# A plan of side pieces between an expert's twelve blocks of matmuls, and the first expert's tables spread over its blocks

## The chip, the core and the metric

One core of a Trainium2 chip runs the whole layer as one program. The metric is the device time of one execution in microseconds. The kernel before takes 2020.53 us, the median of three runs (2020.08 to 2022.52).

## What is computed

One layer over 1024 latent tokens of width 1024 and 256 context tokens: a mixer (gated linear attention and pooling) and then a mixture of 32 experts, four to a token. The change touches the experts alone:

```python
def moe(h, w_router, b_router, w_gu, b_gu, w_down, b_down):
    logits = (xt @ w_router + b_router).astype(jnp.float32)
    top_vals, top_idx = lax.top_k(logits, TOP_K)
    weights = jax.nn.softmax(top_vals, axis=-1)
    ...                                        # tokens sorted by expert, in blocks of 128
    def expert_block(args):
        xblk, e = args
        gu = xblk @ w_gu[e] + b_gu[e]          # 1024 -> 2048
        gate, up = jnp.split(gu, 2, axis=-1)
        gate = jnp.minimum(gate, SWIGLU_LIMIT)
        up = jnp.clip(up, -SWIGLU_LIMIT, SWIGLU_LIMIT)
        act = (up + 1.0) * gate * jax.nn.sigmoid(SWIGLU_ALPHA * gate)
        return act @ w_down[e] + b_down[e]     # 1024 -> 1024
    ...                                        # weighted sum back to the tokens
```

All is float32, and `h + g2 * moe(...)` with a last RMSNorm is the output.

## The kernel before, in words

**Blocks.** An expert's weights are a stream of twelve loads of 1 MB: eight of `w_gu` (128 rows by 2048) and four of `w_down` (256 rows by 1024). SyncE issues them into eight buffers (`ring`, `mix`, `ringx` in the rows). ScalarE rounds each load to `hl[:, 0]` and VectorE writes the remainder to `hl[:, 1]` (`split`, lines 131 and 132), in three `hl` buffers; so the split of a block can start only when TensorE is done with the block three before it. A block of matmuls is then twelve matmuls of 128 by 512 (`gu_chunk` writes `pG`, `dn_chunk` writes `pD`). The eight gate/up blocks of expert e are followed by the four down blocks of expert e-1, and that is one turn of the loop at the end of the listing. The activation of e (`act`, lines 1533 to 1536: `ag` and `at`) is worked out during those four down blocks.

**Heavy and light experts.** An expert has a main set of 128 token slots. The sixteen with the most tokens, here called heavy, have one more set of 32 (the first of them two); the rest are light. A heavy expert's further set adds unsplit matmuls (`pR`) behind its gate/up blocks 3 and 7 and behind its last down block. In the order of work the experts go H H H L L H, then L H twelve times, then L L.

**Side pieces.** Between blocks TensorE does small work for the neighbouring experts: `prep_x` transposes the gathered tokens of the next expert (parts 0 and 1, four transposes each into `pps`, evacuated by a ScalarE copy and a VectorE subtraction into `xT`; part 2, two transposes into `ppr`, evacuated by one ScalarE copy, for a heavy one only), `prep_a` does the same for the activations (`aT`, `aqT`), and `prep_route` finds the token numbers of the expert after next (`pq`) and starts their gather on GpSimd. All of these, and the tables below, share one PSUM bank: the pool `ptr`, tag `t`, one buffer. A piece therefore waits until the piece before it has been evacuated. Before, the pieces stand behind fixed gate/up blocks:

```python
A_AT, X_AT = (0, 2, 3), (4, 6, 7)
```

for the parts 0, 1, 2 of `prep_a` and of `prep_x`; `prep_sel` (VectorE) is written behind block 6, and `prep_route` behind the second down block.

**Start of the experts.** After `prep_x` of the first expert, the bias table (`bias_rows`: three matmuls and a ScalarE copy for each of four quarters), the routing weights (`route_weights`) and the slot weights of two experts follow one after the other, each through the same bank, and then the first block. Behind the first expert's blocks stands `route_blocks`, a chain of small VectorE operations with two small groups of matmuls (`pcs`, `pblk`), and then the second expert begins.

**Order.** A scheduler orders the instructions of VectorE, ScalarE and GpSimd by its own estimate of when each is ready. TensorE's are kept in the order of the program from the expert loop on (`T.strict`).

Of the kernel before, what the change touches and what calls it, by code (L numbers as in the profile page):

```python
# [9 lines left out]
F32 = mybir.dt.float32  # L10
# [4 lines left out]
AF = mybir.ActivationFunctionType  # L15
# [4 lines left out]
P = 128  # L20
D = 1024
KT = D // P
# [4 lines left out]
NE = 32  # L27
# [8 lines left out]
MAXBLK = 32  # L36
# [16 lines left out]
def tile_hybrid_layer(ctx: ExitStack, tc: tile.TileContext, x, c, ctx_in, c_ctx, w_ada, b_ada, norm_mix_w,  # L53
# [9 lines left out]
    V, S, G = nc.vector, nc.scalar, nc.gpsimd  # L63

    def dump(name, ap):
        if name in dbg:
            nc.sync.dma_start(dbg[name], ap)
# [263 lines left out]
    todo = []  # L331
# [895 lines left out]
    def route_weights():  # L1227

        flat = lg.rearrange("p t e -> p (t e)")
        S.activation(lgn, lg, AF.Copy)  # L1230
        G.tensor_tensor(bdg, bdg, g2b[0:96], op=ALU.mult)
        px = ptr.tile([P, 2, P], F32, name="px", tag="t")
        for h in range(2):
            T.transpose(px[:, h], flat[:, h * P:(h + 1) * P], ident)
        wT = tp.tile([P, 2, P], F32, name="wT")
        S.activation(wT, px, AF.Copy)
        py = ptr.tile([P, 2, P], F32, name="pyw", tag="t")
        for h in range(2):
            T.matmul(py[:, h], wT[:, h], pbd.rearrange("p j e -> p (j e)"), start=True, stop=True)
        V.tensor_copy(flat, py.rearrange("p h r -> p (h r)"))  # L1240
        eq = tp.tile([P, NT, NE], F32, name="eq")
        S.activation(info[:, :, :, 2], lg, AF.Copy)
        V.tensor_tensor(eq, lg, info[:, :, :, 2], op=ALU.subtract)
        S.activation(info[:, :, :, 3], eq, AF.Copy)
        V.tensor_tensor(eq, eq, info[:, :, :, 3], op=ALU.subtract)
        S.activation(info[:, :, :, 4], eq, AF.Copy)
        for j in range(4):
            S.activation(g2r[32 * j:32 * j + 32], g2b[32 * j:32 * j + 32, 256 * j:256 * j + 256], AF.Copy)

    def route_blocks():  # L1250

        erb = tp.tile([NE, 2 * NE + 1], F32, name="erb")
        V.tensor_copy(erb[:, 0:NE], pe_[:NE, 0:NE])
        nb = tp.tile([NE, 1], F32, name="nb")
        tmp1 = tp.tile([NE, 1], F32, name="tmp1")
        over = tp.tile([NE, 1], F32, name="over")
        pcs = ptr.tile([NE, 8], F32, name="pcs", tag="t")
        T.matmul(pcs[:, 0:1], eqr[:NE], cnt[:NE], start=True, stop=True)
        V.tensor_tensor(over, pcs[:, 0:1], cap4, op=ALU.subtract)
        for j in range(7):  # L1260
            dst = nb if j == 0 else tmp1
            V.tensor_scalar(dst, over, float(P * j), None, op0=ALU.is_gt)
            if j:
                V.tensor_tensor(nb, nb, tmp1, op=ALU.add)
        pb = ptr.tile([P, 3, NE], F32, name="pblk", tag="t")
        nbb = tp.tile([NE, 2, MAXBLK], F32, name="nbb")
        V.tensor_copy(nbb[:, 0], nb.to_broadcast([NE, MAXBLK]))
        V.tensor_copy(nbb[:, 1], capc.to_broadcast([NE, MAXBLK]))
        T.matmul(pb[:MAXBLK, 0], nbb[:, 0], linc, start=True, stop=True)
        T.matmul(pb[:MAXBLK, 1], nbb[:, 0], ident[:NE, :NE], start=True, stop=True)  # L1270
        T.matmul(pb[:MAXBLK, 2], nbb[:, 1], ident[:NE, :NE], start=True, stop=True)
        inc = tp.tile([MAXBLK, 3, NE], F32, name="inc")
        V.tensor_copy(inc, pb[:MAXBLK])
        V.tensor_copy(nblk1[:, 0:1], inc[0:1, 0, NE - 1:NE])
        V.tensor_scalar(nblk1[:, 1:2], inc[0:1, 0, NE - 1:NE], 1.0, None, op0=ALU.min)
        le = tp.tile([MAXBLK, NE], F32, name="le")
        V.tensor_scalar(le, inc[:, 0], pcol[:MAXBLK], None, op0=ALU.is_le)
        rb_ = tp.tile([MAXBLK, 1], F32, name="rb_")
        V.tensor_reduce(rb_, le, axis=mybir.AxisListType.X, op=ALU.add)
        V.tensor_tensor(le, le, inc[:, 1], op=ALU.mult)  # L1280
        first = tp.tile([MAXBLK, 1], F32, name="first")
        V.tensor_reduce(first, le, axis=mybir.AxisListType.X, op=ALU.add)
        row = tp.tile([MAXBLK, 136], F32, name="row")
        V.memset(row, 0.0)
        V.tensor_scalar(row[:, 0:NE], io[:MAXBLK, 0:NE], rb_, None, op0=ALU.is_equal)
        capb = tp.tile([MAXBLK, 1], F32, name="capb")
        V.tensor_tensor(le, row[:, 0:NE], inc[:, 2], op=ALU.mult)
        V.tensor_reduce(capb, le, axis=mybir.AxisListType.X, op=ALU.add)
        eb = tp.tile([MAXBLK, 1], F32, name="eb")
        V.tensor_tensor(le, row[:, 0:NE], erb[:, 0:NE], op=ALU.mult)  # L1290
        V.tensor_reduce(eb, le, axis=mybir.AxisListType.X, op=ALU.add)
        for i in range(3):
            V.tensor_scalar(row[:, (i + 1) * NE:(i + 2) * NE], io[:MAXBLK, 0:NE], eb, None, op0=ALU.is_equal)
        V.tensor_tensor(first, pcol[:MAXBLK], first, op=ALU.subtract)
        V.scalar_tensor_tensor(row[:, 4 * NE:4 * NE + 1], first, float(P), capb, op0=ALU.mult, op1=ALU.add)
        ebi = tp.tile([MAXBLK, 1], I32, name="ebi")
        V.tensor_copy(ebi, eb)
        nc.scalar.dma_start(ovt, row)
        nc.scalar.dma_start(ove, ebi)
# [11 lines left out]

    bq = ap.tile([P, 4, 512], BF16, name="bq", tag="bq")

    def bias_rows():
        perm = ap.tile([P, 2 * D], BF16, name="perm", tag="y")[:, 0:1536].rearrange(
            "p (a q n j i) -> p a q n j i", a=3, q=4, n=4, j=8)
        V.memset(perm, 0.0)
        for i in range(3):
            V.tensor_copy(perm[:, i, :, :, :, i], pbd.rearrange("p n (q j) -> p q n j", q=4))
        for q in range(4):  # L1320
            pb = ptr.tile([P, 512], F32, name="pbq", tag="t")
            for i in range(3):
                T.matmul(pb, perm[:, i, q].rearrange("p n j i -> p (n j i)"), bt[:, i], start=(i == 0), stop=(i == 2))
            S.activation(bq[:, q], pb, AF.Copy)

    slots = RS + [MS[0], MS[2], MS[3]] + RX

# [64 lines left out]
    def slot_weights(i, pq):  # L1392
        n = 1 + nrem[i]
        wc = xp.tile([P, 3], F32, name="wc", tag="wc", bufs=4)
        V.tensor_reduce(wc[:, :n], pq[:, :n, 2:5], axis=mybir.AxisListType.X, op=ALU.add)
        R["wc", i] = wc

    def prep_route(i):
        pq = ptr.tile([P, 3, 8], F32, name="pq", tag="t")
        route_main(i, pq, slice(0, 5))  # L1400
        route_rem(i, pq, slice(2, 7))
        gather_main(i, pq)
        gather_rem(i, pq)
        slot_weights(i, pq)
# [290 lines left out]
    with tc.high_priority():  # L1695
# [18 lines left out]
        pinned[0] = False  # L1714
        for p_ in range(3):
            prep_x(0, p_)
    bias_rows()
    route_weights()
    dump("posm", posm)
    dump("wfull", lg)  # L1720
    for i in range(2):
        pq = ptr.tile([P, 3, 8], F32, name="pq", tag="t")
        route_main(i, pq, slice(2, 5))
        route_rem(i, pq, slice(2, 5))
        slot_weights(i, pq)
    T.strict = True
    A_AT, X_AT = (0, 2, 3), (4, 6, 7)
    for e in range(nexp + 1):
        if e < nexp:
            gu_start(e)  # L1730
            for k in range(KT):
                advance()
                gu_chunk(e, k)

                if e > 0 and k in A_AT:
                    prep_a(e - 1, A_AT.index(k))
                if e + 1 < NE and k in X_AT:
                    prep_x(e + 1, X_AT.index(k))
                if e + 2 < NE and k == 6:
                    prep_sel(e + 2)  # L1740
                if e + 2 < NE and k == 7 and e == 0:
                    prep_route(e + 2)
        if e > 0:
            dn_start(e - 1)
            for k0 in range(0, KT, 2):
                advance()
                with tc.high_priority() if e == NE - 1 else ExitStack():
                    if k0 == 0 and e < nexp:
                        act(e)
                    if e == NE - 1 and k0 >= 4:  # L1750
                        prep_a(e, k0 // 2 - 2)
                dn_chunk(e - 1, k0)
                if k0 == 2 and e + 2 < NE:
                    prep_route(e + 2)
                if e == NE:
                    (final_tables, lambda: final_weights(0), lambda: final_weights(1), int)[k0 // 2]()
            finish_e(e - 1)
            if e == NE - 1:
                prep_a(e, 2)
                final_rows()  # L1760
        elif nexp:
            act(e)
            route_blocks()
# [149 lines left out]
```

## Time and profile before

| | |
|---|---|
| median of three runs | 2020.53 us |
| profiled execution, its own time | 2023.95 us |
| its span, first to last instruction | 2022.2 us |
| TensorE (PE) busy | 1872.5 us, 93% |
| VectorE (DVE) busy | 1544.6 us, 76% |
| ScalarE (ACT) busy | 1139.1 us, 56% |
| mean granted TensorE clock | 0.971 |

The span is that of one profiled execution, and some 1.8 us lie around it. The experts begin at about 558 us and end at about 1990 us. A share over the whole span mixes the mixer, where TensorE often waits, with the experts, where it seldom does; the rows below are therefore taken from stretches of the experts. In a timeline row, the bracket at the end is the idle time of the engine just before the row, with what ended it.

### The profile page before, as it was taken

Reading aid. Unit: us, or ns where it says so; the run is one execution under the profiler, and the core shown is the slowest. Engines: PE = TensorE matmul, PEld = TensorE weight load, DVE = VectorE, ACT = ScalarE, POOL = GpSimd, SP = SyncE. Lnnn points to the kernel's source line nnn. Section 1 sums busy time; section 2 is a strip of 40 time slices with the busy share of each in tenths; the row PEclk is TensorE's granted clock in tenths of the full one; section 3 lists DMA queues with packets and bytes.
Section 4 is the critical chain, followed back from the end, with each engine's and each line's share of the span. In section 5 each row is a group of like instructions: output and inputs, shape, how many; then the busy total and the mean of one; then the engine's idle time right before and its main releaser. Section 6 shows DMA issues by size and latency. Waiting matters only on the chain.

```text
span 2022.2 us, 29473 instructions
## 1 busy us (share of the span) xinstructions
PE 1872.5 (93%) x11472; PEld 1373.6 (68%) x11473; DVE 1544.6 (76%) x1606; ACT 1139.1 (56%) x1267; POOL 339.0 (17%) x238
## 2 busy tenths in 40 slices
PE   7999998999389999999999999999999999999995
PEld 4776776787256677767677676767667676767774
DVE  5486478658667788878788788878878887887887
ACT  4564456644435566656566565656656565665664
POOL 2010043011300221111111111111111111111114
PEclk9999998999599999999999999999999999999998
DMA  9285422243635789968888796888879688887985
GB/s 343 78 295 180 152 75 92 77 151 134 237 159 199 285 327 332 357 248 355 297 317 326 283 367 246 348 305 316 324 286 366 246 343 302 322 324 290 365 305 178
DMA packets 125528, 532.33 MB, mean 263 GB/s; under 512 B 13196, under 2 KB 27328, under 8 KB 90568
## 3 DMA queue, kind: packets, MB, share of 16 engines
q1 hardware_dynamic: 109464, 481.82, 61.2%
q0 software_dynamic: 15344, 48.01, 9.1%
q8 instruction: 92, 1.51, 0.3%
q10 hardware_dynamic: 576, 0.56, 0.1%
q14 instruction: 52, 0.43, 0.1%
HBM read 497.68 MB, written 32.67 MB: 262 GB/s over the span
## 4 chain that ended last, share of the span: by engine, by line
PE 78%; DVE 9%; ACT 5%; issue 4%; DMA 3%; POOL 1%; SPq 0%; POOLq 0%; DVEq 0%; ACTq 0%
PE pG L74 31%; PE pD L74 17%; PE pa L74 12%; PE pR L74 9%; ACT hl L131 4%; DVE hl L132 3%; PE pw L74 2%; PE pps L79 2%; PE pt L74 2%; DMA ringx<-in_w_down_dram 1%; PE pt L79 1%; PE ppr L79 1%; PE pDl L74 1%; PE pq L74 1%; DVE xT L1413 1%
## 5 line engine op out<-in xcount | busy, mean ns | idle before, releaser
L74 PE MATMUL pG<-hl,xT 128*128 128x512 f32 x3072 | 769.2, 402 | 0.0
L74 PEld LDWEIGHTS pG<-hl,xT 128*128 128x128 f32 x3072 | 566.0, 189 | 144.3 <-issue 21.9
L132 DVE TENSOR_TENSOR hl<-ring,hl 128x2048 fp32r<-128x2048 f32 (+2 forms) x199 | 398.4, 2009 | 168.9 <-ACT hl L131 167.4
L131 ACT ACTIVATE hl<-ring 128x2048 fp32r<-128x2048 f32 (+2 forms) x199 | 331.9, 1670 | 304.2 <-PE pG L74 168.2
L132 DVE TENSOR_TENSOR hl<-mix,hl 128x2048 fp32r<-128x2048 f32 x144 | 329.5, 2290 | 121.8 <-ACT hl L131 121.8
L131 ACT ACTIVATE hl<-mix 128x2048 fp32r<-128x2048 f32 (+1 forms) x146 | 277.7, 1902 | 234.4 <-PE pG L74 168.7
L74 PE MATMUL pD<-hl,aT 128*128 128x512 f32 x1488 | 365.5, 401 | 0.3 <-DVE hl L132 0.3
L74 PEld LDWEIGHTS pD<-hl,aT 128*128 128x128 f32 x1488 | 276.6, 189 | 76.0 <-issue 11.7
L132 DVE TENSOR_TENSOR hl<-ringx,hl 128x2048 fp32r<-128x2048 f32 x96 | 219.7, 2288 | 24.5 <-ACT hl L131 24.2
L131 ACT ACTIVATE hl<-ringx 128x2048 fp32r<-128x2048 f32 x96 | 184.0, 1917 | 93.0 <-PE pG L74 54.5
L1374 POOL DMA_INDIRECT xg<-h2d,ix x32 | 64.4, 2012 | 884.3 <-DVE ix L1370 424.8
L74 PE MATMUL pa<-hl,hi 128*128 128x512 f32 x544 | 180.4, 417 | 5.7 <-DVE wsg L760 3.7
L1588 POOL DMA_INDIRECT acc<-y,ix x31 | 104.5, 3369 | 156.8 <-DVE y L1583 156.8
L74 PEld LDWEIGHTS pa<-hl,hi 128*128 128x128 f32 x544 | 102.5, 197 | 31.4 <-DVE wsg L760 4.8
L74 PE MATMUL pa<-hl,lo 128*128 128x512 f32 x272 | 107.7, 407 | 0.0
L74 PE MATMUL pa<-hi,hl 128*128 128x512 f32 (+1 forms) x288 | 95.6, 395 | 1.0 <-ACT hi L400 1.0
L74 PEld LDWEIGHTS pa<-hi,hl 128*128 128x128 f32 x288 | 54.9, 193 | 16.2 <-ACT hi L400 2.9
L1593 POOL DMA_INDIRECT acc<-yq,ixr x17 | 34.0, 1999 | 163.5 <-DMA acc<-y,ix 150.1
L74 PEld LDWEIGHTS pa<-hl,lo 128*128 128x128 f32 x272 | 52.8, 196 | 11.9 <-issue 1.1
L74 PE MATMUL pa<-lo,hl 128*128 128x512 f32 (+1 forms) x144 | 55.3, 387 | 1.8 <-DVE lo L401 1.8
L74 PE MATMUL pR<-ring,xqT 128*32 128x512 f32 x408 | 53.3, 596 | 0.0
L1534 ACT ACTIVATE ag<-ag 128x1024 f32<-128x1024 f32 (+1 forms) x49 | 40.7, 831 | 20.7 <-DVE ag L1533 20.7
(392 smaller groups left out, 2031.2 us busy)
## 6 DMA issues: line engine op xcount, KB each, us to landing
ring<-in_w_gu_dram SPq DMA_DIRECT2D x96, 1024.0 KB, 15.3
mix<-in_w_gu_dram SPq DMA_DIRECT2D x96, 1024.0 KB
ringx<-in_w_gu_dram SPq DMA_DIRECT2D x64, 1024.0 KB, 6.8
ring<-in_w_down_dram SPq DMA_DIRECT2D x48, 1024.0 KB
mix<-in_w_down_dram SPq DMA_DIRECT2D x48, 1024.0 KB, 18.6
ringx<-in_w_down_dram SPq DMA_DIRECT2D x32, 1024.0 KB, 16.5
ring<-in_w_in_dram SPq DMA_DIRECT2D x32, 512.0 KB, 5.4
ring<-in_w_ada_dram SPq DMA_DIRECT2D x16, 1024.0 KB, 5.8
```

The lines of the kernel that those rows point to most:

```text
L74: i = nc.tensor.matmul(*a, **k)
L79: i = nc.tensor.transpose(*a, **k)
L131: S.activation(hl[:, 0], src, AF.Copy)
L132: i = eng.tensor_tensor(hl[:, 1], src, hl[:, 0].bitcast(F32), op=ALU.subtract)
L1374: nc.gpsimd.indirect_dma_start(out=xg, out_offset=None, in_=h2d, in_offset=bass.IndirectOffsetOnAxis(ap=ix[:, 0:1], axis=0))
L1413: V.tensor_tensor(dst[:, 1, part], pp, dst[:, 0, part].bitcast(F32), op=ALU.subtract)
L1534: S.activation(g, g, AF.Gelu_apprx_sigmoid)
L1588: nc.gpsimd.indirect_dma_start(out=acc, out_offset=bass.IndirectOffsetOnAxis(ap=ix[:, 0:1], axis=0), in_=y, in_offset=None, compute_op=ALU ...
L1593: nc.gpsimd.indirect_dma_start(out=acc4, out_offset=bass.IndirectOffsetOnAxis(ap=ixr[g][:, 0:1], axis=0), in_=yq, in_offset=None, compute_ ...
```

## The change

The two tuples go. A function `plan(e)` says which pieces stand behind each of the twelve blocks of a turn, 0 to 7 being gate/up blocks and 8 to 11 down blocks: from the second expert on `prep_a` at 0, 2, 4, `prep_x` at 5, 7, 9, `prep_sel` at 8 and `prep_route` at 10. For the first expert the plan holds the tables that stood ahead of it, and `route_blocks` is cut into `route_counts` and `route_rows`, which stand behind blocks of the second expert, as does the last quarter of the bias table. The functions themselves compute what they computed.

```diff
-        A_AT, X_AT = (0, 2, 3), (4, 6, 7)
+    perm = bias_perm()
...
+    def plan(e):
+        todo = {}
+
+        def at(k, f, *a):
+            todo.setdefault(k, []).append((f, a))
+        if e == 0:
+            for k, q in ((0, 0), (2, 2), (4, 1)):
+                at(k, bias_rows, perm, q)
+            at(1, route_weights)
+            at(3, prep_x, 1, 2)
+            at(5, weigh, 0)
+            at(5, weigh, 1)
+            at(6, prep_x, 1, 0)
+            at(7, prep_x, 1, 1)
+            at(7, prep_sel, 2)
+            return todo
+        if e == NE:
+            return todo
+        for k, p in ((0, 0), (2, 1), (4, 2)):
+            at(k, prep_a, e - 1, p)
+        if e + 1 < NE:
+            for k, p in ((5, 0), (7, 1), (9, 2)):
+                at(k, prep_x, e + 1, p)
+        if e == 1:
+            at(1, prep_route, 2)
+            at(3, route_counts)
+            at(6, route_rows)
+            at(11, bias_rows, perm, 3)
+        if e + 2 < NE:
+            at(8, prep_sel, e + 2)
+            at(10, prep_route, e + 2)
+        return todo
...
             for k in range(KT):
                 advance()
                 gu_chunk(e, k)
-                if e > 0 and k in A_AT:
-                    prep_a(e - 1, A_AT.index(k))
-                if e + 1 < NE and k in X_AT:
-                    prep_x(e + 1, X_AT.index(k))
...
+                extras(k)
...
                 dn_chunk(e - 1, k0)
-                if k0 == 2 and e + 2 < NE:
-                    prep_route(e + 2)
+                if e < nexp:
+                    extras(KT + k0 // 2)
...
-            act(e)
-            route_blocks()
```

(`extras(k)` calls what the plan holds for place k; `weigh(i)` is the body of the loop over the two experts' slot weights that stood ahead of the experts.)

TensorE in a light expert between two heavy ones, from its gate/up block 2 on, before (`aT` parts are `pps<-ident,at`, the activations' further set is `ppr<-ident,at`, the tokens' is `ppr<-ident,xq`):

```order
L74 MATMUL pG<-hl,xT 128x512 x12
L79 MATMUL pps<-ident,at 128x128 x4
L74 MATMUL pG<-hl,xT 128x512 x12
L79 MATMUL ppr<-ident,at 128x128 x2
L74 MATMUL pG<-hl,xT 128x512 x12
L79 MATMUL pps<-ident,xg_10390 128x128 x4
L74 MATMUL pG<-hl,xT 128x512 x24
L79 MATMUL pps<-ident,xg_10390 128x128 x4
L74 MATMUL pG<-hl,xT 128x512 x12
L79 MATMUL ppr<-ident,xq 128x128 x2
L74 MATMUL pD<-hl,aT 128x512 x24
```

and now:

```order
L74 MATMUL pG<-hl,xT 128x512 x12
L79 MATMUL pps<-ident,at 128x128 x4
L74 MATMUL pG<-hl,xT 128x512 x24
L79 MATMUL ppr<-ident,at 128x128 x2
L74 MATMUL pG<-hl,xT 128x512 x12
L79 MATMUL pps<-ident,xg_10406 128x128 x4
L74 MATMUL pG<-hl,xT 128x512 x24
L79 MATMUL pps<-ident,xg_10406 128x128 x4
L74 MATMUL pD<-hl,aT 128x512 x24
L79 MATMUL ppr<-ident,xq 128x128 x2
L74 MATMUL pD<-hl,aT 128x512 x12
```

Each `ppr` had one block (x12) between itself and the `pps` ahead of it, and has two now (x24); the first `pps<-ident,xg` has one block behind a `ppr`, and the second stands right ahead of the down blocks.

VectorE in such a light expert, from its seventh split on, before (`hl` are splits, `xT` the evacuation of a token piece, `ag` and `at` the activation):

```order
L132 TENSOR_TENSOR hl<-mix,hl 128x2048
L132 TENSOR_TENSOR hl<-ringx_4706,hl 128x2048
L1413 TENSOR_TENSOR xT<-pps,xT 128x512
L1533 TENSOR_SCALAR ag<-pG 128x1024
L1535 TENSOR_SCALAR at<-pG 128x1024
L132 TENSOR_TENSOR hl<-ringx_4707,hl 128x2048
L1536 SCALAR_TENSOR_TENSOR at<-at,ag 128x1024
L132 TENSOR_TENSOR hl<-ring_71,hl 128x2048
```

and now:

```order
L1423 TENSOR_TENSOR xT<-pps,xT 128x512
L132 TENSOR_TENSOR hl<-ringx_4706,hl 128x2048
L1543 TENSOR_SCALAR ag<-pG 128x1024
L1545 TENSOR_SCALAR at<-pG 128x1024
L132 TENSOR_TENSOR hl<-ringx_4707,hl 128x2048
L1423 TENSOR_TENSOR xT<-pps,xT 128x512
L1546 SCALAR_TENSOR_TENSOR at<-at,ag 128x1024
L132 TENSOR_TENSOR hl<-ring_71,hl 128x2048
```

The second `xT` stood ahead of `ag`, `at` and a split, and stands behind all three now.

TensorE at the start of the experts, before (`pbq` is the bias table, `px` and `pyw` the routing weights, `pG` the first blocks):

```order
L79 MATMUL ppr<-ident,xq 128x128 x4
L74 LDWEIGHTS perm
L74 MATMUL pbq<-mix,perm 128x512
...
L79 MATMUL px<-ident,lg 128x128 x2
L74 MATMUL pyw<-pbd,wT 128x128 x2
...
L74 MATMUL pG<-hl,xT 128x512 x48
```

and now:

```order
L79 MATMUL ppr<-ident,xq 128x128 x4
L74 MATMUL pG<-hl,xT 128x512 x12
L74 LDWEIGHTS perm
L74 MATMUL pbq<-mix,perm 128x512
...
L74 MATMUL pG<-hl,xT 128x512 x12
L79 MATMUL px<-ident,lg 128x128 x2
L74 MATMUL pyw<-pbd,wT 128x128 x2
L74 MATMUL pG<-hl,xT 128x512 x12
```

The first block stands right behind the first expert's transposes, and the tables between it and the blocks that follow.

## Rows read from the trace of the kernel before

**Rows 1.** The page, part 1: busy time of each engine.

```profile
span 2022.2 us, 29473 instructions
PE 1872.5 (93%) x11472; PEld 1373.6 (68%) x11473; DVE 1544.6 (76%) x1606; ACT 1139.1 (56%) x1267; POOL 339.0 (17%) x238
```

**Rows 2.** Waits of TensorE, 600 to 1960 us: in total, times, longest.

```profile
PE ppr L79 <- DVE aT L1413: 23.8, 14, 1.7
PE ppr L79 <- DVE xT L1413: 22.5, 13, 2.1
PE pblk L74 <- DVE nbb L1267: 3.6, 1, 3.6
```

**Rows 3.** Windows, a light and a heavy expert: stretch, length, busy, PEclk, DMA, GB/s.

```profile
1011.10:1055.20 44.10, 40.70 (x242) 30.74 (x240) 39.15 (x26) 28.69 (x20) 6.22 (x4) 1.00 0.80 307
1055.20:1099.30 44.10, 44.10 (x279) 31.14 (x277) 33.35 (x27) 24.38 (x17) 8.19 (x4) 1.00 0.87 319
```

**Rows 4.** Timeline of TensorE in that light expert: start, length, operation, [idle before].

```profile
1025.50 0.44 PE L79 MATMUL ppr<-ident,at 128*128 128x128 f32 x2 [1.70 <-DVE aT L1413]
...
1028.94 5.83 PE L74 MATMUL pG<-hl,xT 128*128 128x512 f32 x24
1034.61 0.60 PE L79 MATMUL pps<-ident,xg 128*128 128x128 f32 x4
1034.97 3.04 PE L74 MATMUL pG<-hl,xT 128*128 128x512 f32 x12
1039.71 0.44 PE L79 MATMUL ppr<-ident,xq 128*128 128x128 f32 x2 [1.70 <-DVE xT L1413]
```

**Rows 5.** Timeline of ScalarE, same light expert.

```profile
1034.81 1.92 ACT L131 ACTIVATE hl<-ringx 128x2048 fp32r<-128x2048 f32 x1 [0.88 <-PE pG L74]
...
1040.18 0.38 ACT L1419 ACTIVATE xqT<-ppr 128x256 f32<-128x256 f32 x1 [0.23 <-PE ppr L79]
```

**Rows 6.** Timeline of VectorE, same light expert.

```profile
1036.76 2.29 DVE L132 TENSOR_TENSOR hl<-ringx,hl 128x2048 fp32r<-128x2048 f32 x1 [0.50 <-ACT hl L131]
1038.97 0.68 DVE L1413 TENSOR_TENSOR xT<-pps,xT 128x512 fp32r<-128x512 f32 x1
1039.57 1.22 DVE L1533 TENSOR_SCALAR ag<-pG 128x1024 f32<-128x1024 f32 x1
1040.70 1.22 DVE L1535 TENSOR_SCALAR at<-pG 128x1024 f32<-128x1024 f32 x1
1041.83 2.29 DVE L132 TENSOR_TENSOR hl<-ringx,hl 128x2048 fp32r<-128x2048 f32 x1
```

**Rows 7.** Timeline of TensorE in the last light expert but one.

```profile
1926.33 5.63 PE L74 MATMUL pD<-hl,aT 128*128 128x512 f32 x23 [0.34 <-DVE hl L132]
```

**Rows 8.** Timeline of TensorE in the fifth expert.

```profile
777.19 0.44 PE L79 MATMUL ppr<-ident,xq 128*128 128x128 f32 x2 [2.07 <-DVE xT L1413]
777.38 7.39 PE L74 MATMUL pD<-hl,aT 128*128 128x512 f32 x24
```

**Rows 9.** Windows, just behind that wait (columns as in rows 3).

```profile
777.80:781.20 3.40, 3.40 (x10) 2.63 (x9) 3.40 (x3) 1.31 (x2) 0.00 (x0) 0.50 1.01 424
```

**Rows 10.** Timeline of TensorE, first and second expert.

```profile
538.55 0.69 PE L79 MATMUL ppr<-ident,xq 128*128 128x128 f32 x2 [1.39 <-ACT xqT L1419]
...
557.96 13.62 PE L74 MATMUL pG<-hl,xT 128*128 128x512 f32 x48
...
598.54 0.44 PE L79 MATMUL ppr<-ident,xq 128*128 128x128 f32 x2
...
605.02 0.31 PE L74 MATMUL pblk<-linc,nbb 32*32 32x32 f32 x2 [3.64 <-DVE nbb L1267]
...
605.47 5.35 PE L74 MATMUL pG<-hl,xT 128*128 128x512 f32 x12
```

**Rows 11.** Windows, from the first transposes to the first block (columns as in rows 3).

```profile
539.00:558.00 19.00, 9.26 (x132) 4.26 (x130) 6.23 (x7) 8.42 (x10) 0.00 (x0) 0.50 0.69 286
```

**Rows 12.** Windows, down blocks of the light expert of rows 4 (columns as in rows 3).

```profile
1046.00:1050.00 4.00, 4.00 (x18) 3.23 (x18) 4.00 (x5) 2.88 (x2) 1.78 (x1) 1.00 0.00 0
```

More of the change, by code (lines that the diff above doesn't have):

```diff
@@ L1248, in route_weights, with route_counts @@
             S.activation(g2r[32 * j:32 * j + 32], g2b[32 * j:32 * j + 32, 256 * j:256 * j + 256], AF.Copy)
+    B = {}
     def route_blocks():
-        erb = tp.tile([NE, 2 * NE + 1], F32, name="erb")
+        erb = B["erb"] = tp.tile([NE, 2 * NE + 1], F32, name="erb")
         V.tensor_copy(erb[:, 0:NE], pe_[:NE, 0:NE])
+    def route_counts():
         nb = tp.tile([NE, 1], F32, name="nb")
@@ L1264, in route_blocks, with route_rows @@
                 V.tensor_tensor(nb, nb, tmp1, op=ALU.add)
-        pb = ptr.tile([P, 3, NE], F32, name="pblk", tag="t")
-        nbb = tp.tile([NE, 2, MAXBLK], F32, name="nbb")
+        nbb = B["nbb"] = tp.tile([NE, 2, MAXBLK], F32, name="nbb")
         V.tensor_copy(nbb[:, 0], nb.to_broadcast([NE, MAXBLK]))
         V.tensor_copy(nbb[:, 1], capc.to_broadcast([NE, MAXBLK]))
+    def route_rows():
+        nbb, erb = B["nbb"], B["erb"]
+        pb = ptr.tile([P, 3, NE], F32, name="pblk", tag="t")
         T.matmul(pb[:MAXBLK, 0], nbb[:, 0], linc, start=True, stop=True)
@@ L1312, in tile_hybrid_layer, with bias_perm @@
     bq = ap.tile([P, 4, 512], BF16, name="bq", tag="bq")
-    def bias_rows():
+    def bias_perm():
         perm = ap.tile([P, 2 * D], BF16, name="perm", tag="y")[:, 0:1536].rearrange(
@@ L1319, in bias_rows @@
             V.tensor_copy(perm[:, i, :, :, :, i], pbd.rearrange("p n (q j) -> p q n j", q=4))
[L1320 to L1324, printed above, removed]
+        return perm
+    def bias_rows(perm, q):
+        pb = ptr.tile([P, 512], F32, name="pbq", tag="t")
+        for i in range(3):
+            T.matmul(pb, perm[:, i, q].rearrange("p n j i -> p (n j i)"), bt[:, i], start=(i == 0), stop=(i == 2))
+        S.activation(bq[:, q], pb, AF.Copy)
     slots = RS + [MS[0], MS[2], MS[3]] + RX
@@ L1716, in tile_hybrid_layer, with weigh @@
             prep_x(0, p_)
[L1717 to L1721, printed above, removed]
+    perm = bias_perm()
+    def weigh(i):
         pq = ptr.tile([P, 3, 8], F32, name="pq", tag="t")
@@ L1725, in tile_hybrid_layer, with extras @@
         slot_weights(i, pq)
+    def plan(e):
[29 more added lines that the diff above has]
+        return todo
     T.strict = True
-    A_AT, X_AT = (0, 2, 3), (4, 6, 7)
     for e in range(nexp + 1):
+        todo = plan(e)
+        def extras(k):
+            for f, a in todo.pop(k, ()):
+                f(*a)
         if e < nexp:
@@ L1733, in tile_hybrid_layer @@
                 gu_chunk(e, k)
-                if e > 0 and k in A_AT:
-                    prep_a(e - 1, A_AT.index(k))
-                if e + 1 < NE and k in X_AT:
-                    prep_x(e + 1, X_AT.index(k))
-                if e + 2 < NE and k == 6:
-                    prep_sel(e + 2)
-                if e + 2 < NE and k == 7 and e == 0:
-                    prep_route(e + 2)
+                extras(k)
         if e > 0:
@@ L1752, in tile_hybrid_layer @@
                 dn_chunk(e - 1, k0)
-                if k0 == 2 and e + 2 < NE:
-                    prep_route(e + 2)
+                if e < nexp:
+                    extras(KT + k0 // 2)
                 if e == NE:
```

## The prediction

> **What bounds the kernel now.** I read the busy times first: TensorE works 1872.5 us of a span of 2022.2 us, VectorE 1544.6 and ScalarE 1139.1 [rows 1]. Then TensorE's waits in the stretch of the experts: nearly all of its idle time there stands in two rows, 23.8 us in 14 waits and 22.5 us in 13, both ahead of the small transposes `ppr` and both ended by VectorE [rows 2]. The windows of two neighbouring experts say where: in the heavy one TensorE is busy 44.10 of 44.10 us, in the light one 40.70 of 44.10 [rows 3]. The two waits of 1.70 us in its timeline are those 3.40 us [rows 4]. So TensorE sets the time here, and in a pair of 88.2 us it loses 3.4 us at the PSUM bank that the pieces share: `ppr` may not write it until VectorE has evacuated the `pps` one block earlier.
>
> The other loss is the beginning. The first expert's transposes end at 539.2 (538.55 + 0.69), its first block starts at 557.96. Behind it another 6.9 us pass, from 598.54 to the second expert's first block at 605.47 [rows 10]. In the first of these stretches the granted clock is 0.50, TensorE's lower level of 1.2 GHz, and TensorE is busy 9.26 of 19.00 us [rows 11].
>
> **The change, part by part.** The sum is made against the profiled execution, 2023.95 us (span 2022.2 and about 1.8 around it); the median of the runs, 2020.53, is 3.4 lower, and I take the same saving off it.
>
> *The activations' `ppr`, from one block behind a `pps` to two.* A block is 2.84 us: two run from 1028.94 to 1034.61 [rows 4]. Evacuating a `pps` takes, from the end of the block ahead of it: 0.20 until ScalarE takes up a split (1034.61 to 1034.81), 1.92 for that split [rows 5], 2.21 for VectorE's half (1036.76 to 1038.97) and 0.68 for the evacuation [rows 6], 5.0 in all. One block and the transposes themselves (0.36, from 1034.61 to 1034.97) give 3.2 us, hence a wait of 1.8 in this count and 1.70 in the row; two blocks give 6.0. All 14 waits go: -23.8 us. What is late next: the first `pps` of the tokens now stands one block behind this `ppr`. Its evacuation is ScalarE's copy alone, 0.38 us, behind one split at worst: 0.20 + 1.92 + 0.38 = 2.5, against 2.84. I take 0; the bounds are 0 and 0.6 each (another copy in front), 8 us in all.
>
> *The tokens' `ppr`, from gate/up block 7 to the second down block.* It too is two blocks behind its `pps`, but VectorE's row has changed there: the evacuation stands behind a split, `ag`, `at` and another split. From the end of gate/up block 6: 0.20 + 1.92 + 2.21 + 1.13 + 1.13 + 2.21 + 0.68 = 9.5 us, the steps read from one start to the next [rows 5, 6]. TensorE comes to `ppr` after a block, a `pps` and two blocks: 2.84 + 0.36 + 5.68 = 8.9. So about 0.6 us of wait stays in each of 13 places: 22.5 - 7.8 = 14.7 saved. Bounds: no wait (7.8 more saved), or the whole of the old one (14.7 less). The third down block's split stands ahead of that evacuation and so is ready with it; the fourth block's split is ready about as TensorE gets there (0 to 0.34 us each, the latter being what the one light expert without a token `ppr` waits for its split [rows 7]; 4 us in all). I take 0, and give that one 0.34 back, since its split no longer stands behind an `xT`: -0.3.
>
> *The clock behind the longest wait.* In the fifth expert the wait is 2.07 us, and the next 3.40 us are granted 0.50 [rows 8, 9]. The 24 matmuls behind it take 7.39 instead of 5.7. With a wait of 0.6 that goes: -1.7.
>
> *The beginning.* TensorE gets 18.7 us (539.2 to 557.96) and 6.9 us (598.54 to 605.47) back, and the block of 5.35 us that ran cold behind the latter becomes 3.04 as a warm one [rows 4, 10]: 27.9. The pieces still have to be done between blocks: half of 9.26 at the full clock is 4.6, and the 6.9 hold some 1.7 besides three waits, of which 3.64 is the longest; left are 21.6. New waits come in, since several of these pieces stand one block apart, or none. The routing weights' second half waits for a copy behind a split on ScalarE: 0.20 + 1.92 + 0.38 less the 0.35 of the transposes, 2.15. In the second expert `pq` behind block 1 and `pblk` behind block 6 each stand one block behind a `pps`, 1.8 each as above; the second of two `ppr` behind block 4 waits for a copy behind a split, 2.3; some 0.3 more between the slot weights. Together 8.4, so 13.2 us are left. Each of the four long ones is near the 2.07 us that was followed by a slow clock: I let two of them cost 1.7, leaving -9.8. Bounds: 21.6 (nothing waits) and 0. The blocks themselves have their weights: the loads run ahead, and `hl` of the first block is ready before its transposes.
>
> This is the place where I weigh a rule. Rows: in the window of a light expert two waits of 1.70 us left the clock at 1.00 [rows 3, 4], the one of 2.07 did not [rows 8, 9]. The Trainium skill, "TensorE: Matmul & The Clock Gate", section "A second HAM failure mode: psum-queue depth-cycling", says that short pauses of TensorE between groups of matmuls, from cycling through PSUM banks, come often enough to send the clock up and down, so that each group pays. Taken at its word all four new waits would pay, 6.8 for 3.4, and the time would be 1973.6; the trace agrees with it at one wait and not at the 26 shorter ones.
>
> *On other queues.* Gather and `prep_sel` move with `prep_route` by one down block, and the tokens' first transposes by one block too, so the gather has the same seven blocks. SyncE's loads keep their order; in the light expert's down blocks the DMA queues even run empty, 0 GB/s in 4 us [rows 12].
>
> Sum: 23.8 + 14.7 + 0.3 + 1.7 + 9.8 = 50.3. The profiled execution would come to 1973.6, the median to **1970 us**.
>
> **The rivals.**
>
> *VectorE takes the place of the bank.* It is busy 39.15 of the light expert's 44.10 us [rows 3]; in 40.7 that would be 96%. For it: the order above, where evacuation and splits queue behind the activation, and the late split [rows 7]. Against: the heavy expert leaves it 10.75 us idle, so a lag ends there. If the token waits stay whole and each pair loses a split's 0.34 as well, 14.7 + 4.4 come back: 1989; if the activations' waits returned too, 2009.
>
> *The first expert's spread gives nothing*, its waits and the lower clock eating the 21.6: 1980.
>
> *The loads become the bound.* A pair keeps the DMA busy 0.80 and 0.87 of its halves [rows 3], 74 of 88 us, and a pair would shrink by 2.8. For it: bursts at 424 GB/s [rows 9]. Against: the empty 4 us [rows 12], more than the pair loses. Price: the 38.5 of the experts, 2009.
>
> *No change*: the first two in full, 1970 + 38.5 + 9.8 = 2018.8.
>
> *Slower: the waits move and each now drops the clock.* If the evacuations in the new order come so late that all 27 places wait 2.07 us as in rows 8, each costs 2.07 + 1.7, 102 us, instead of the 48 of now (23.8 + 22.5 + 1.7): 54 more, less the 9.8 of the beginning, 2064. It decides from waits of 2.07 on; for it speaks that VectorE's evacuation does move back, against it that the count above gives 0.6. The section of the Trainium skill named above describes such a clock.
>
> **How the numbers follow.** Forecast 0.70 (its own range 1956 to 1984: 7.8 less or 7 more at the token waits, some 9 either way at the beginning, seldom all at once); VectorE 0.14 (1985 to 2009); nothing from the first expert 0.07; loads 0.02; no change 0.03; slower 0.04. A measurement of this kernel tells 0.2%, 4 us, from nothing. Faster: 0.70 + 0.14 + 0.07 + 0.02 = 0.93; same 0.03; slower 0.04. The range 1956 to 1990 holds the forecast, the weak first expert and half of VectorE's case.
>
> **What would show it.** The row of 23.8 us gone from TensorE's waits, that of 22.5 down to about 8, as 13 waits near 0.6 behind the second down block; a pair of some 85.4 us instead of 88.2; the heavy window still full; no half-clock window at the fifth expert; first block near 539, second expert's near 588, and four waits of about 2 us in these two. Wrong would be: waits for `hl` of more than a few us in all, token waits of 1.7 or more, DMA as a releaser of ScalarE's splits in the light experts, or a first block that again starts near 558.

## The result, and the profile after

The changed kernel takes **1967.8 us**, the median of four runs (1964.62 to 1971.5); the kernel before took 2020.34 beside it. The ratio is 0.9738, with an interval of 0.9715 to 0.9762. The forecast was 1970.

The profiled execution took 1964.81 us; the four took 1964.62, 1964.81, 1970.8 and 1971.5. The page of after, part 1:

```profile
span 1963.0 us, 29497 instructions
...
PE 1859.0 (95%) x11470; PEld 1368.7 (70%) x11473; DVE 1544.2 (79%) x1606; ACT 1136.8 (58%) x1267; POOL 352.7 (18%) x238
```

Beside [rows 1] the span is 59.2 us shorter. TensorE's busy time fell by 13.5, so some 46 us of its idle time are gone; VectorE's busy time is the same in a shorter span. The waits of TensorE in after, 600 to 1910 us (total, times, longest), answer to [rows 2]:

```profile
PE ppr L79 <- DVE xT L1423: 7.3, 13, 0.6
PE pps L79 <- DVE at L1546: 3.8, 1, 3.8
PE ppr L79 <- ACT aqT L1429: 2.1, 1, 2.1
PE pblk L74 <- DVE xT L1423: 1.7, 1, 1.7
PE pD L74 <- DVE hl L132: 1.1, 2, 0.9
```

The row of 23.8 us is gone, that of 22.5 is 7.3, still 13 waits but of 0.6 us. (The 3.8 is the last expert's; the kernel before has one like it, later than the window of [rows 2].) The `ppr` of 2.1 and the `pblk` of 1.7 are the second expert's.

Windows of a light and of a heavy expert in after, columns as in rows 3:

```profile
984.28:1025.28 41.00, 40.44 (x241) 30.80 (x239) 38.15 (x25) 28.36 (x20) 10.05 (x4) 1.00 0.81 313
1025.28:1069.41 44.13, 44.13 (x280) 31.18 (x277) 34.37 (x28) 24.61 (x17) 6.37 (x4) 1.00 0.91 335
```

The light expert takes 41.00 us where it took 44.10 [rows 3], the heavy one is full as before. TensorE's timeline in this light expert, to be read against [rows 4]:

```profile
999.64 0.38 PE L79 MATMUL ppr<-ident,at 128*128 128x128 f32 x2
...
1002.65 0.60 PE L79 MATMUL pps<-ident,xg 128*128 128x128 f32 x4
1003.01 5.84 PE L74 MATMUL pG<-hl,xT 128*128 128x512 f32 x24
1008.68 0.60 PE L79 MATMUL pps<-ident,xg 128*128 128x128 f32 x4
1009.03 5.84 PE L74 MATMUL pD<-hl,aT 128*128 128x512 f32 x24
1015.44 0.44 PE L79 MATMUL ppr<-ident,xq 128*128 128x128 f32 x2 [0.56 <-DVE xT L1423]
```

The activations' `ppr` has no bracket: it waits for nothing. Nor does the first `pps` of the tokens behind it. The tokens' `ppr` waits 0.56 us for `xT`. VectorE in the same stretch shows why:

```profile
1008.03 2.29 DVE L132 TENSOR_TENSOR hl<-ringx,hl 128x2048 fp32r<-128x2048 f32 x1 [0.34 <-ACT hl L131]
1010.24 1.22 DVE L1543 TENSOR_SCALAR ag<-pG 128x1024 f32<-128x1024 f32 x1
1011.38 1.21 DVE L1545 TENSOR_SCALAR at<-pG 128x1024 f32<-128x1024 f32 x1
1012.51 2.28 DVE L132 TENSOR_TENSOR hl<-ringx,hl 128x2048 fp32r<-128x2048 f32 x1
1014.71 0.68 DVE L1423 TENSOR_TENSOR xT<-pps,xT 128x512 fp32r<-128x512 f32 x1
```

The evacuation starts at 1014.71, although its `pps` ended at 1009.28 and ScalarE's half of it was written by 1011.27: a split, the two halves of the activation and another split stand ahead of it without a gap. It ends at 1015.39, and TensorE has been waiting since 1014.88.

The first two experts in after (TensorE's timeline), to be read against [rows 10]:

```profile
535.47 0.69 PE L79 MATMUL ppr<-ident,xq 128*128 128x128 f32 x2 [1.28 <-ACT xqT L1429]
535.80 4.21 PE L74 MATMUL pG<-hl,xT 128*128 128x512 f32 x12
...
546.05 0.71 PE L74 MATMUL pyw<-pbd,wT 128*128 128x128 f32 x4 [2.36 <-ACT wT L1236]
546.51 3.04 PE L74 MATMUL pG<-hl,xT 128*128 128x512 f32 x12
...
582.96 3.04 PE L74 MATMUL pG<-hl,xT 128*128 128x512 f32 x12
...
590.93 0.64 PE L74 MATMUL pq<-info,sel 128*128 128x5 bf16 x40 [1.70 <-DVE aT L1423]
591.49 3.06 PE L74 MATMUL pG<-hl,xT 128*128 128x512 f32 x12
...
607.33 0.44 PE L79 MATMUL ppr<-ident,at 128*128 128x128 f32 x2 [2.05 <-ACT aqT L1429]
607.53 3.04 PE L74 MATMUL pG<-hl,xT 128*128 128x512 f32 x12
...
615.49 0.24 PE L74 MATMUL pblk<-linc,nbb 32*32 32x32 f32 x2 [1.70 <-DVE xT L1423]
...
615.79 4.60 PE L74 MATMUL pG<-hl,xT 128*128 128x512 f32 x12
```

The first block follows its transposes at once, at 535.80 (557.96 before), the second expert's first block stands at 582.96 (605.47 before). Four new waits of 2.36, 1.70, 2.05 and 1.70 us came in. Of these four, only the last was followed by a lower clock: the block behind it takes 4.60 us, those behind the other three 3.04 to 3.06. (The first block, 4.21 us, begins at the lower clock, which the waits among the first transposes leave.) Two windows of after (columns as in rows 3), behind that wait and behind the fifth expert's token `ppr`, where [rows 9] stand for before:

```profile
616.90:620.30 3.40, 3.40 (x9) 2.19 (x7) 1.84 (x6) 0.00 (x0) 0.00 (x0) 0.50 0.00 0
...
763.70:767.10 3.40, 3.40 (x24) 2.62 (x23) 3.40 (x3) 1.83 (x3) 0.00 (x0) 1.00 1.02 419
```

The first is granted half the clock, the second all of it, where before had 0.50.

**Where the 59.2 us went.** By the starts of the experts' first blocks in the two timelines: 3.1 us lie ahead of everything the change touches (the first expert's last transposes start at 538.55 before, at 535.47 after); from there to the third expert's first block 13.2; from the third to the sixth expert 4.6; the twelve pairs behind it 37.05, 3.09 each; the end 1.3. The 3.1 I count to the executions and not to the change: the first transposes of the experts, `pps`, stand at 531.39 before, at 528.42 in after, and between 528.25 and 530.90 in the five experiments below, and VectorE's copy to `posm`, still further ahead of everything that was changed, stands at 522.49 before and at 519.58 in after. With one trace for each kernel that isn't shown further. It is part of why the medians lie 52.5 us apart and not 59.

### The profile page after: what moved, and what is told of

Read it like the earlier page. It is cut to its first block, busy times and chain, and to the rows that moved or that the text cites. A ratio compares the mean times of both kernels' runs of the same rounds, so it can differ in the third digit from the quotient of the medians.

```text
span 1963.0 us, 29497 instructions
## 1 busy us (share of the span) xinstructions
PE 1859.0 (95%) x11470; PEld 1368.7 (70%) x11473; DVE 1544.2 (79%) x1606; ACT 1136.8 (58%) x1267; POOL 352.7 (18%) x238
## 4 chain that ended last, share of the span: by engine, by line
PE 78%; DVE 9%; issue 5%; ACT 4%; DMA 2%; POOL 1%; SPq 0%; DVEq 0%; POOLq 0%; ACTq 0%
PE pG L74 34%; PE pD L74 13%; PE pa L74 12%; PE pR L74 9%; PE pps L79 3%; ACT hl L131 3%; DVE hl L132 2%; PE pw L74 2%; PE pt L74 1%; DVE ag L1543 1%; DVE at L1545 1%; PE pt L79 1%; DMA mix<-in_w_gu_dram 1%; PE pDl L74 1%; DVE xT L1423 1%
## 5 line engine op out<-in xcount | busy, mean ns | idle before, releaser
L1384 POOL DMA_INDIRECT xg<-h2d,ix x32 | 79.9, 2498 | 881.1 <-DVE wc L1405 842.8
```

The source lines that it names most:

```text
L1384: nc.gpsimd.indirect_dma_start(out=xg, out_offset=None, in_=h2d, in_offset=bass.IndirectOffsetOnAxis(ap=ix[:, 0:1], axis=0))
```

## The experiments

The theory: the saving is two separate things, the time that TensorE loses at the shared bank (some 40 us, by the spacing of the pieces and by what stands ahead of an evacuation on VectorE), and the beginning (some 10). The rivals: the spread alone carries most of it; the tokens' new place matters little; the rest that waits is of another cause.

**The spacing alone.** The new places from the second expert on; the first expert's tables ahead of its blocks as in the kernel before.

```diff
+    for q in range(4):
+        bias_rows(perm, q)
+    route_weights()
...
+    weigh(0)
+    weigh(1)
...
-            at(1, route_weights)
-            at(3, prep_x, 1, 2)
-            at(5, weigh, 0)
-            at(5, weigh, 1)
-            at(6, prep_x, 1, 0)
-            at(7, prep_x, 1, 1)
-            at(7, prep_sel, 2)
+            for k, p in ((4, 0), (6, 1), (7, 2)):
+                at(k, prep_x, 1, p)
+            at(6, prep_sel, 2)
+            at(7, prep_route, 2)
...
+            route_counts()
+            route_rows()
```

> The new places of the pieces from the second expert on, but the first expert's tables ahead of the blocks as before. Theory (the waits at the shared bank are the larger term): the spacing alone is worth 12 pairs of 3.1 us and some 4 us at experts 2 to 4, so 1979 us, pairs of 85.1 us, activation waits gone and 13 token waits near 0.6 us. Rival (most of the gain is the beginning, and the new VectorE order hides a loss in the experts): 2000 us or more.

Measured: 1981.55 us (1979.69 to 1983.42), 0.9801 of the kernel before [0.9785, 0.9818]. Its waits of TensorE, 600 to 1910 us:

```profile
PE ppr L79 <- DVE xT L1423: 7.3, 13, 0.6
PE pblk L74 <- DVE nbb L1270: 3.7, 1, 3.7
```

The first row is that of after to the digit, the second is the wait of the old beginning [rows 2]. Spacing alone is worth 39.5 us (2021.08 beside it).

**The first expert's spread alone.** The old places from the third expert on.

```diff
-        for k, p in ((0, 0), (2, 1), (4, 2)):
+        for k, p in ((0, 0), (2, 1), (4 if e == 1 else 3, 2)):
-            for k, p in ((5, 0), (7, 1), (9, 2)):
+            for k, p in ((5, 0), (7, 1), (9, 2)) if e == 1 else ((4, 0), (6, 1), (7, 2)):
-            at(8, prep_sel, e + 2)
-            at(10, prep_route, e + 2)
+            at(8 if e == 1 else 6, prep_sel, e + 2)
+            at(10 if e == 1 else 9, prep_route, e + 2)
```

> The first expert's tables spread, the second expert as changed, the old places from the third expert on. Theory: 13 us less than before, 2007 us, with pairs of 88.2 us and 27 waits of 1.7 us as before; this and the kernel with the spacing alone add up to the change. Rival (the spread only shifts idle time into the first two experts): 2015 to 2020 us.

Measured: 2010.42 us (2007.94 to 2013.88), 0.9944 [0.9924, 0.9963]. Its waits of TensorE, 600 to 1910 us:

```profile
PE ppr L79 <- DVE aT L1423: 23.8, 14, 1.7
PE ppr L79 <- DVE xT L1423: 22.2, 13, 1.7
```

Both rows of [rows 2] are back, but for the longest wait of the second. The spread is worth 10.7 us, where after has 13.0 more than the spacing alone (52.5 less 39.5); the two parts sum to 50.2 of 52.5. The 2.3 us between them lie within the intervals, which are 3 us and more to either side for each of the three kernels, so the parts add up as far as these runs can tell. The profiled executions do differ in one place: the first two experts of this run are those of after, with the same four waits (2.05 where after has 2.36), but TensorE's timeline shows a block at the lower clock behind each of them:

```profile
546.85 1.22 PE L74 MATMUL pyw<-pbd,wT 128*128 128x128 f32 x4 [2.05 <-ACT wT L1236]
547.72 4.22 PE L74 MATMUL pG<-hl,xT 128*128 128x512 f32 x12
...
593.30 0.63 PE L74 MATMUL pq<-info,sel 128*128 128x5 bf16 x40 [1.70 <-DVE aT L1423]
593.87 4.61 PE L74 MATMUL pG<-hl,xT 128*128 128x512 f32 x12
...
611.24 0.44 PE L79 MATMUL ppr<-ident,at 128*128 128x128 f32 x2 [2.05 <-ACT aqT L1429]
611.43 4.59 PE L74 MATMUL pG<-hl,xT 128*128 128x512 f32 x12
...
620.95 0.24 PE L74 MATMUL pblk<-linc,nbb 32*32 32x32 f32 x2 [1.70 <-DVE xT L1423]
...
621.25 4.60 PE L74 MATMUL pG<-hl,xT 128*128 128x512 f32 x12
```

Four blocks of 4.2 to 4.6 us in place of 3.04, where after has one: three more, some 4.3 us in this execution. Whether that is what separates the medians isn't shown.

**The tokens' `ppr` one block earlier.** Behind the first down block, so one block behind its `pps` in place of two; everything else as after.

```diff
-            for k, p in ((5, 0), (7, 1), (9, 2)):
+            for k, p in ((5, 0), (7, 1), (9 if e == 1 else 8, 2)):
```

> The changed kernel with the tokens' small transposes one block earlier, behind the first down block instead of the second, from the third expert on. Theory (TensorE waits until VectorE has done a split, ag, at, another split and then the evacuation, 9.5 us behind gate/up block 6, and comes there after 6.0 us now): 13 waits of 3.4 us instead of 0.6, 37 us more, 2005 us; if each such wait also lets the clock fall, 1.7 us more at each, up to 2027 us. Rival (the scheduler's order adapts and VectorE evacuates in time): within 5 us of the changed kernel, 1968 us.

Measured: 2030.41 us (2025.45 to 2032.74), 1.0041 of the kernel before [1.0031, 1.0051]: one block in 13 places, and the whole change is lost and more. Its waits of TensorE, 600 to 1910 us, and TensorE's timeline in a light expert:

```profile
PE ppr L79 <- DVE xT L1423: 43.7, 13, 3.4
```

```profile
1029.74 0.69 PE L79 MATMUL ppr<-ident,xq 128*128 128x128 f32 x2 [3.36 <-DVE xT L1423]
1030.09 6.94 PE L74 MATMUL pD<-hl,aT 128*128 128x512 f32 x24
```

The wait is 3.36 us, 2.8 more than in after, as one block fewer of 2.84 us gives. The 24 matmuls behind it take 6.94 us where after has 5.84, and this window says why:

```profile
1029.20:1032.60 3.40, 2.85 (x8) 2.38 (x9) 3.40 (x3) 0.38 (x1) 0.00 (x0) 0.51 0.15 63
```

The clock is granted at half. So it goes behind all 13 of these waits: the 24 matmuls take 6.94 to 7.39 us in nine places and 8.24 to 8.43 in four, and the light experts take 45.1 to 46.5 us where after has 41.0. Of the 60.7 us between the two spans 36.4 are waits (43.7 less 7.3); nearly all of the rest, 22.8, is the longer time of the 24 matmuls in the 13 places, which is the clock. This is the mechanism of the prediction's slower rival, waits that each drop the clock, brought about by one step of the place.

**The tokens' `ppr` ahead of its `pps`.** From the third expert on the tokens' pieces stand in the order `ppr`, `pps`, `pps`, so that only ScalarE's copy stands between the `ppr` and the next piece, and the last evacuation has until the next expert.

```diff
-            for k, p in ((5, 0), (7, 1), (9, 2)):
+            for k, p in ((5, 0), (7, 1), (9, 2)) if e == 1 else ((5, 2), (6, 0), (8, 1)):
```

> The changed kernel with the order of a light expert's token pieces turned round from the third expert on: the small ppr at 5 (its bank is freed by ScalarE's copy alone), the two pps at 6 and 8. Theory: VectorE's chain now ends where only pq waits for it, behind the third down block: 12.3 us against 12.1 behind gate/up block 6, so waits of 0.2 to 0.4 us instead of 0.6; 3 to 5 us less than the changed kernel, 1964 us. Rival (VectorE itself is the bound in a light expert, 39 of 41 us): no gain, the 0.6 us come back as waits for a split.

Measured: 1961.1 us (1960.19 to 1964.51), 0.9703 [0.9686, 0.9721], a saving of 60.0 us, 7.4 more than after's, though the two intervals just overlap. TensorE's timeline in a light expert:

```profile
1005.15 0.38 PE L79 MATMUL ppr<-ident,xq 128*128 128x128 f32 x2
...
1008.16 0.60 PE L79 MATMUL pps<-ident,xg 128*128 128x128 f32 x4
...
1014.54 6.00 PE L74 MATMUL pD<-hl,aT 128*128 128x512 f32 x24
```

No row has a bracket, and the row of 13 waits is gone; the light expert takes 40.50 us where after has 41.00, and a pair 84.66 for 85.13, so the twelve pairs, 4.8 us together, account for most of the gain. The 0.6 that were left in after are therefore the evacuation behind the activation, as the prediction counted, and not the transposes. They are not wholly gone: the two down blocks take 6.00 us where after has 5.84, and `pq` follows their start by 5.98 (at 1020.52), where in after a piece follows the start of two blocks by 5.67 (1003.01 to 1008.68). These 0.3 us are what the expectation left. One block behind a `ppr` is enough, two are needed behind a `pps`.

**The first two experts in the same manner.** This is the version that the runs pointed to; "the last run" in its expectation is the experiment above. `spare` is a PSUM bank that is free until the second expert's down blocks; parts 3 and 4 are the two halves of a part 2, `route_weights2` is `pyw` and what follows.

```diff
+            R["spare"] = r1[:, 1]
...
-            for k, q in ((0, 0), (2, 2), (4, 1)):
+            at(0, prep_x, 0, 3)
+            at(0, prep_x, 0, 4)
+            for k, q in ((1, 0), (2, 1), (4, 2), (5, 3)):
                 at(k, bias_rows, perm, q)
             at(1, route_weights)
+            at(2, route_weights2)
...
-        for k, p in ((0, 0), (2, 1), (4, 2)):
+        for k, p in ((0, 0), (2, 1), (3, 3), (4, 4)) if e == 1 else ((0, 0), (2, 1), (4, 2)):
...
```

> The order of the last run (token pieces with ppr first) for all experts, and no two pieces one block apart in the first two: the first expert's second pps in a bank of its own, its two ppr behind the first block, px and pyw one block apart, the second expert's two activation ppr one block apart, and the bias table, pq of the third expert and pcs, pblk in a bank that is free until the second expert's down blocks. Theory (each of these waits is lost time of TensorE, and two of them cost a stretch at half clock): by the last run's rows the first block comes 4.3 us earlier (537.6 to 532.3 less two ppr behind it), the waits of 2.05, 1.70, 0.32, 2.05 and 1.69 us go, 7.8 in all, and the blocks of 4.40 and 4.61 us become 3.04 and 3.06, 2.9: 15.0 us in all, 1946 us. Rival (the loads or the splits cannot follow so early, and waits for hl take the place): 1956 us or more, with waits of pG for hl in the first two experts.

Measured: 1948.48 us (1945.33 to 1950.96), 0.9637 of the kernel before [0.9624, 0.965], the fastest of all, and 2.5 above the 1946 expected. TensorE's timeline from the first transposes on:

```profile
530.90 1.94 PE L79 MATMUL pps<-ident,xg 128*128 128x128 f32 x8 [3.37 <-DMA xg<-h2d,ix]
532.73 4.85 PE L74 MATMUL pG<-hl,xT 128*128 128x512 f32 x12
...
537.77 0.48 PE L74 MATMUL pG<-hl,xT 128*128 128x512 f32 x1
539.96 2.83 PE L74 MATMUL pG<-hl,xT 128*128 128x512 f32 x11 [1.71 <-DVE hl L132]
```

The waits of the first two experts at the bank are gone, and with them the half clock behind two of them: from the first transposes to the third expert's first block it takes 102.5 us (530.90 to 633.42) where the run before took 117.2 (529.70 to 646.85). That is 14.7 us less, with 15.0 expected. What the rival said came true in one place: behind its first matmul the second block waits 1.71 us until its weights are split. This wait lies inside the 14.7, so it isn't what puts the measured time 2.5 us above the expected one: in these two executions the first transposes stand 1.2 us later, and the stretch behind the third expert's first block is 0.9 longer (1313.7 us against 1312.8).

## Why the prediction was right, point by point

**The sum.** The median came out 2.2 us under the forecast, but the sum was made against the profiled execution, and there 59.1 us were saved (2023.95 to 1964.81) where it counts 50.3. Of the 8.8 us between, 3.1 lie ahead of the change, 3.4 are the beginning (13.2 for 9.8), and 2.4 the experts from the third on (42.95 for 40.5). In these, the busy time of a pair is 0.23 us shorter, 2.8 us in twelve pairs, which the sum doesn't have. So the mechanism was right term by term, and that the median was hit within 2.2 us is in part luck with the executions.

**The activations' `ppr`, -23.8.** Right, to the row. Nor is the `pps` behind it late (bound 0 to 8): at 1002.65 it shows no bracket in after.

**The tokens' `ppr`, -14.7.** Right: 13 waits of 0.56 us where the count gave 0.6, so 15.2 saved. The order of VectorE's row, read without a time, and the durations of [rows 5, 6] were enough for it; the two runs with the `ppr` elsewhere show that it is this queue that decides.

**The late split, -0.3.** Wrong in sign and without weight: that wait for a split went from 0.34 [rows 7] to 0.89 us. The prediction took it that this split no longer stands behind an `xT`. On VectorE it stands behind an `xT` and the last step of the activation, and ScalarE takes it up behind a copy of `xT` and the activation's `ag`. A light expert with a token `ppr` has the 0.56 us in front and doesn't show it.

**The clock at the fifth expert, -1.7.** Right: with a wait of 0.56 in that place, a window of after at 1.00 stands where [rows 9] have 0.50.

**The pair, 85.4.** It is 85.13 (41.00 + 44.13). The waits give 2.84 of the 3.1 us (3.40 less 0.56), as counted; the rest is TensorE's busy time, 84.57 where [rows 3] have 84.80.

**The beginning, -9.8.** The mechanism was right, the size low in the profile, 13.2; the two experiments give 10.7 and 13.0, with intervals that hold 9.8 too. The four waits came as listed, 2.36, 1.70, 2.05 and 1.70 against 2.15, 1.8, 2.3 and 1.8. Mis-sized was the clock: two of them were to cost 1.7 each, in the profile of after one did (4.60 us for a block of 3.04, 1.6), in executions of three other kernels with the same places none, two and four. Two was a fair middle; that the number varies the prediction didn't see. The remaining 1.7 us of the 13.2 (11.5 with one drop) I can't put down to one place. An estimate for some 0.9 of it: the first four blocks of before, 13.62 us, run some 2.1 longer than four blocks at 2.84 us would, since they begin at the lower clock; the first block of after loses only 1.2 in that way (4.21 for 3.04).

**The rule on the clock.** Taken at its word, the section "A second HAM failure mode: psum-queue depth-cycling" of "TensorE: Matmul & The Clock Gate" in the Trainium skill would have let all four new waits pay. The traces agree with it in the run with the spread alone, where all four did, and for the 13 waits of 3.36 us with the tokens' `ppr` one block earlier; they don't for the first two experts of that same run, where none of the four did, nor in after, where one of four did and none of the 13 of 0.56 us.

**The rivals.** VectorE took nobody's place: it is busy 38.15 of 41.00 us in the light window, and 40.50 us were reached with the same work. The loads are no bound at 40.50 either, where no row of TensorE waits. The weak first expert and the slower case didn't come about in after, though the slower case lies one block away, and it took waits of 3.36 us, well beyond the 2.07 from which the prediction let it decide.

## What to carry to other kernels

Where small pieces on TensorE share one PSUM bank, count the distance of two pieces in blocks against the evacuation's whole way: what stands ahead of it in the queues of ScalarE and VectorE, not its own 0.68 us. A piece that one engine copies out needs one block here, and one that passes two engines needs two. With the activation in the queue even two are 0.6 us short (0.3 in the other order); whether a third would clear that no run tried. So put the quick one first and the slow one ahead of the longest gap. A place that is wrong by one block cost more here than the whole change brought, since the longer wait also took the clock.

## What the runs showed of the hardware

The drop of the granted clock from 1.00 to 0.50 doesn't go by the length of the wait alone, nor by the pieces ahead of it in the program. The same four places of the first and the second expert's blocks (`pyw`, `pq`, the second `ppr`, `pblk`) waited 2.36, 1.70, 2.05 and 1.70 us in after and dropped it once, behind the last; with the tokens' `ppr` first they waited 2.05, 1.70, 2.05 and 1.69 and dropped it twice, behind the third and the fourth:

```profile
608.98 0.69 PE L79 MATMUL ppr<-ident,at 128*128 128x128 f32 x2 [2.05 <-ACT aqT L1429]
609.32 4.40 PE L74 MATMUL pG<-hl,xT 128*128 128x512 f32 x12
...
618.64 0.24 PE L74 MATMUL pblk<-linc,nbb 32*32 32x32 f32 x2 [1.69 <-DVE xT L1423]
...
618.95 4.61 PE L74 MATMUL pG<-hl,xT 128*128 128x512 f32 x12
```

With the first expert's spread alone, behind waits of 2.05, 1.70, 2.05 and 1.70 us, they dropped it four times. With the tokens' `ppr` one block earlier the waits are the same four to the digit and dropped it not once: the blocks behind them take 3.04, 3.06, 3.04 and 3.07 us, at a granted clock of 1.00. In the experts from the third on, 26 waits of 1.70 us in the kernel before left it at 1.00 and all 13 of 3.36 us dropped it in the run that had them. The 26 are not quite the same case as the four, where small matmuls follow some of the waits: from the end of a block to the start of the next pass 1.9 us at the 26, 2.0 to 3.1 at the four, 3.7 at the 13. So a pause of 2 to 3 us between blocks may or may not cost a block at the lower clock, and one execution doesn't tell which; what decides it stays open, and no run here takes it apart. It may have a part in the spread of after's executions: the two of 1964.6 and 1964.8 us have mean granted clocks of 0.978 and 0.977, those of 1970.8 and 1971.5 of 0.973 and 0.974. Only one of the four has a trace.
